# A decoder trunk on one core: a third pair of SwiGLU units by block products, and SiLU in one step

## The chip, the cores and the metric

One core of one Trainium2 chip runs the whole program in one launch. The metric is the device time of one execution in microseconds; smaller is better. Three runs of the kernel before were timed, and one more execution was profiled.

## What is computed

Four layers. Each is: half a SwiGLU, a token mixer (retention, sparse attention with an indexer, native sparse attention, retention) beside a four-head attention into 256 memory tokens, and half a SwiGLU again. There are 256 tokens of width 1024, all float32, and the hidden width of a SwiGLU is 2816. Only the SwiGLU is touched:

```python
def swiglu(x, wg, wu, wd):
    return (jax.nn.silu(x @ wg) * (x @ wu)) @ wd

h = rms_norm(x, ffn_norm[i, 0])
x = x + 0.5 * swiglu(h, ffn_w_gate[i, 0], ffn_w_up[i, 0], ffn_w_down[i, 0])
```

## The kernel before

**Tiles and precision.** The 256 tokens are two row tiles `t` of 128. Every matrix product is done three times in a reduced-precision float32 type (F32R): an operand is split into `hi`, a rounded copy made on ScalarE, and `lo`, the rest, a subtraction on VectorE. `mm3` (L307 to L311) multiplies hi by hi, hi by lo and lo by hi. Weights are split on the chip too: each raw block of 128 x 2048 becomes two halves of 128 x 1024 (`split`, L281 and L282).

**Units.** A SwiGLU's weights come in units, in the order of `FFN_ORDER` (L23): gate/up units `("g", u)`, each 1024 x 512 (256 gate columns and 256 up columns), and down units `("d", u)`, each 512 x 1024 (the last 256 x 1024). An ordinary unit has two raw blocks of 1 MB. Both row tiles use a unit one after the other: 48 matmuls of 512 columns.

**Pairs by block products.** For each `u` in `JOINT` (L26; 4 and 8), units `u` and `u + 1` are one "j" unit of four blocks b11, b21, b12, b22. The two row tiles, the two halves of the inner dimension and the two units form a 2 x 2 block product, which `joint` (L477) does in seven products in place of eight: 84 matmuls (lines L491 to L493) in place of 96, with sums of blocks before and sums of products after. The sums of the token side are made once per SwiGLU (`sums`, L431) and held as five `op` tiles until its last pair. `fetch_joint` (L211) builds t1 = b12 + b11: SP loads the two halves of b12 into `sum` tiles, and POOL's DMA adds b11 onto them as it lands (L229). Then b11, b22 and b21 are loaded plain. `split_joint` (L237) splits seven blocks into 14 halves, in the order b11, t1, t2, t3, b21, t4, b22, each by a copy on ScalarE (L253) and a subtraction on VectorE (L254). t2 = t1 + b22 and t4 = t2 + b21 are summed in place (L250). t3 = t2 - b11 is put into two `sum` tiles of its own (L247).

**Buffers.** There are three raw buffers (8 KB a partition), nine pairs of `hi`/`lo` halves (`HALVES`), nine 4 KB buffers with the tag a4, which `sum` and `op` tiles share, and two banks of PSUM each for `pg` and for `pj`/`pT`.

**What sets the order.** `load` (L182) chains all loads of weights on SP: each is issued after the one before it in the code, whichever buffer it waits for. Units are fetched and split in the order of the list; in each `tick` one or two halves are split. Within these bounds the program's order on each engine is fixed when it is built.

**After a gate/up unit** (`ffn`, L1244): with p holding gate and up columns, r the row's 1/rms and rh = r/2, r2 = r squared, ScalarE computes `th = tanh(rh * gate)` (L1265), VectorE `th = (th + 1) * gate` (L1266) and `h = th * r2 * up` (L1271). The factor of 2 that this leaves is taken back at the end of the SwiGLU, with 0.25 for 0.5 (L1298). Every two units, h is transposed and split into `hTh` and `hTl` (L1280, L1281), the operands of the down units. The order of a SwiGLU is then g0 to g3, d0, pair 4/5, d1, g6, g7, d2, pair 8/9, d3, g10, d5, d4.

Of the kernel before, what the change touches and what calls it, by code (L numbers as in the profile page):

```python
# [11 lines left out]
AF = mybir.ActivationFunctionType  # L12
OP = mybir.AluOpType
# [9 lines left out]
FFN_ORDER = [("g", 0), ("g", 1), ("g", 2), ("g", 3), ("d", 0), ("g", 4), ("g", 5), ("d", 1),  # L23
             ("g", 6), ("g", 7), ("d", 2), ("g", 8), ("g", 9), ("d", 3), ("g", 10), ("d", 5), ("d", 4)]

JOINT = (4, 8,)  # L26


C_CS, C_TRI, C_GI, C_DK, C_CM, C_ANY, C_CCS, C_BM = 0, 256, 384, 390, 396, 524, 525, 653
# [51 lines left out]
class Net:  # L81
# [48 lines left out]
    def plan(self):  # L130
        a = self.a

        def ffn(i, j):
            for kind, u in FFN_ORDER:
                if kind == "g" and u in JOINT:
                    self.units.append(("j", [a["gu"][i, j, u, 0], a["gu"][i, j, u, 1], a["gu"][i, j, u + 1, 0],
                                             a["gu"][i, j, u + 1, 1]], None))
                elif kind == "g" and u - 1 in JOINT:
                    continue
# [15 lines left out]
        for j, i in enumerate(self.layers):  # L155
            n = len(self.units)
            ffn(i, 0)
            for u in range(n, len(self.units)):
                both(u)
            if j == 0:  # L160
                memory(i)
            kind = i % 3
            names = {0: ["ret"] * 5, 1: ["dsa0", "dsa1", "dsa2", "dsa2"],
                     2: ["nsa0", "nsa0", "nsa0", "nsa1", "nsa2", "nsa3"]}[kind]
            seen = {}
            for n in names:
                u = seen[n] = seen.get(n, -1) + 1
                w = a[n]
                idx = (i // 3, u) if n == "ret" else (u,)
                self.units.append(("w", [w[idx + (0,)], w[idx + (1,)]], None))  # L170
                both(len(self.units) - 1)
            if j + 1 < len(self.layers):
                memory(self.layers[j + 1])
            for u in range(2):
                self.units.append(("w", [a["wout"][i, u, 0], a["wout"][i, u, 1]], None))
            n = len(self.units)
            self.seq += [(n - 2, 0), (n - 1, 0), (n - 2, 1), (n - 1, 1)]
            ffn(i, 1)
            for u in range(n, len(self.units)):
                both(u)  # L180
# [56 lines left out]
    def split_joint(self, u):  # L237
        nc = self.nc
        raw, parts = self.raw.pop(u), self.parts[u]
        parts.update({n: [] for n in ("b11", "t1", "t2", "t3", "b21", "t4", "b22")})  # L240
        half = lambda n, q: raw[n][:, 1024 * q:1024 * q + 1024] if n[0] == "b" else raw[n][q]

        def quarter(name, src, q, plus):
            x = half(src, q)
            if name == "t3":
                raw.setdefault("t3", []).append(self.t4([128, 1024], "sum"))
                nc.vector.tensor_sub(raw["t3"][q], x, half("b11", q))  # L247
                x = raw["t3"][q]
            elif plus:
                nc.vector.tensor_add(x, x, half(plus, q))  # L250
            hi = self.wp.tile([128, 1024], F32R, name="hi", tag="hi", bufs=HALVES)
            lo = self.wp.tile([128, 1024], F32R, name="lo", tag="lo", bufs=HALVES)
            nc.scalar.activation(hi, x, AF.Copy)  # L253
            nc.vector.tensor_sub(lo, x, hi.bitcast(F32))  # L254
            parts[name].append((hi, lo))

        for name, src, plus in (("b11", "b11", None), ("t1", "t1", None), ("t2", "t1", "b22"), ("t3", "t1", None),
                                ("b21", "b21", None), ("t4", "t1", "b21"), ("b22", "b22", None)):
            for q in range(2):
                self.splits.append((u, lambda name=name, src=src, q=q, plus=plus: quarter(name, src, q, plus)))  # L260
# [983 lines left out]
    def ffn(self, t, g, st):  # L1244

        nc = self.nc
        H, acc, nd = {}, None, 0
        X = self.X[t]
        for kind, ui in FFN_ORDER:
            u = yield  # L1250
            if not H:
                s, r, rh, r2 = st["n"]
            if kind == "g":
                r_, rh_, r2_ = r, rh, r2
                if u == 0:
                    p = self.first[t]
                elif isinstance(u, tuple):
                    p, (_, r_, rh_, r2_) = u
                else:
                    p = self.pB("pg")  # L1260
                    self.project(p, s, u)
                if t and ui == 0:
                    self.sums()
                th = self.t1([128, 256], "th")
                nc.scalar.activation(th, p[:, :256], AF.Tanh, scale=rh_)  # L1265
                nc.vector.scalar_tensor_tensor(th, th, 1.0, p[:, :256], op0=OP.add, op1=OP.mult)  # L1266

                if ui % 2 == 0:
                    h = self.t2([128, 512], "h")
                hs = h[:, ui % 2 * 256:ui % 2 * 256 + 256]  # L1270
                nc.vector.scalar_tensor_tensor(hs, th, r2_, p[:, 256:], op0=OP.mult, op1=OP.mult)  # L1271
                if ui % 2 or ui == 10:
                    n = 4 if ui % 2 else 2
                    hl = H[ui // 2] = [self.t2([128, 4, 128], f"hT{x}", F32R) for x in "hl"]

                    def turn(h=h, hl=hl, n=n):
                        c = self.pC("pT")
                        for k in range(n):
                            nc.tensor.transpose(c[:, k], h[:, k * 128:k * 128 + 128], self.ident)  # L1279
                        nc.scalar.activation(hl[0][:, :n], c[:, :n], AF.Copy)  # L1280
                        nc.vector.tensor_sub(hl[1][:, :n], c[:, :n], hl[0][:, :n].bitcast(F32))  # L1281

                    self.later(WAIT["h"], turn)
            else:
                pr = self.parts[u]
                if acc is None:
                    acc = self.pA("acc")
                nk = len(pr)
                for cb in range(2):
                    for k in range(nk):  # L1290
                        hl = H[ui]
                        wh, wl = pr[k]
                        o = cb * 512
                        self.mm3(acc[cb], hl[0][:, k], hl[1][:, k], wh[:, o:o + 512], wl[:, o:o + 512],
                                 nd == 0 and k == 0, nd == 5 and k == nk - 1)
                    if nd == 5:
                        xs = X[:, cb * 512:cb * 512 + 512]
                        nc.vector.scalar_tensor_tensor(xs, acc[cb], 0.25, xs, op0=OP.mult, op1=OP.add)  # L1298
                        if g is None:
                            nc.scalar.dma_start(self.a["out"][t * 128:(t + 1) * 128, cb * 512:cb * 512 + 512], xs)  # L1300
                        else:
                            (self.norm_half if g >= 8 else self.norm_kept)(t, g, cb, st)
                    if cb == 0:
                        self.tick()
                nd += 1
        if g is not None:
            self.norm_stats(t, st)
# [303 lines left out]
```

## Time and profile before

| what | value |
| --- | --- |
| median of 3 runs | 2041.11 us (2036.3 to 2041.76) |
| the profiled execution | 2034.82 us |
| its span, first to last instruction | 2033.0 us |
| TensorE, VectorE, ScalarE busy | 99%, 76%, 55% of the span |
| mean granted clock of TensorE | 0.998 of full speed |
| read from HBM | 365.84 MB |

The busy time of an engine is the union of its instructions' times. Matmuls are pipelined: a matmul of 512 columns shows as about 0.39 us, while the next one begins some 0.23 us after it, so paces are read from stretches and not from single matmuls. PEld is TensorE's weight load, which overlaps the matmuls. DVE, ACT, POOL and SP are VectorE, ScalarE, GpSimd and SyncE; SPq and POOLq mark DMAs that they issue. An arrow with a name, as in `<-ACT hi L253`, names what ended the idle time before an instruction.

### The profile page before, as it was taken

What the parts mean: (1) busy time and instruction counts of PE and PEld (TensorE: products, weight loads), DVE (VectorE), ACT (ScalarE), POOL (GpSimd) and SP (SyncE); (2) the same over time, 40 slices, a digit from 0 to 9 for tenths busy, and PEclk for the clock granted to TensorE, in tenths of its full rate; (3) what the DMA queues carried; (4) which work ended last, traced back from release to release, by engine and by line L of the source; (5) the groups of instructions that cost most, each with busy time, mean ns of one, the idle gap of its engine ahead of it and who ended that gap; (6) DMA issues with size and microseconds to landing.
All of it is one profiled execution on the core that took longest, in us unless ns stands there. A gap on an engine that the chain in (4) does not pass through costs nothing.

```text
span 2033.0 us, 25241 instructions
## 1 busy us (share of the span) xinstructions
PE 2004.1 (99%) x9486; PEld 1615.2 (79%) x9486; DVE 1554.8 (76%) x2241; ACT 1114.5 (55%) x1562; POOL 198.5 (10%) x317
## 2 busy tenths in 40 slices
PE   8999999999999999999999999999999999999999
PEld 6777777888888787888788788878888878778887
DVE  7877756888787787887788876668887878657875
ACT  5545555556555555655555554555555646545553
POOL 0000402000001022100000113220000000301000
PEclk9999999999999999999999999999999999999999
DMA  6656535565545533655556553135655566435553
GB/s 246 221 187 228 187 117 194 165 229 222 192 186 178 203 114 125 205 189 169 218 193 232 188 179 131 67 110 202 217 197 186 166 228 223 150 125 199 194 166 125
DMA packets 57770, 368.53 MB, mean 181 GB/s; under 512 B 6576, under 2 KB 6992, under 8 KB 18864
## 3 DMA queue, kind: packets, MB, share of 16 engines
q1 hardware_dynamic: 51696, 347.76, 46.3%
q0 software_dynamic: 4800, 17.19, 4.8%
q10 hardware_dynamic: 1152, 1.97, 0.3%
q8 instruction: 75, 1.23, 0.2%
q14 instruction: 47, 0.39, 0.1%
HBM read 365.84 MB, written 1.05 MB: 180 GB/s over the span
## 4 chain that ended last, share of the span: by engine, by line
PE 87%; DMA 5%; DVE 4%; ACT 1%; issue 1%; POOL 1%; SPq 0%; ACTq 0%; POOLq 0%; DVEq 0%
PE pg L309 8%; PE pg L311 8%; PE pg L310 8%; PE acc L310 8%; PE acc L311 8%; PE acc L309 8%; DMA sum<-gu 4%; PE pg L492 3%; PE pg L491 3%; PE pg L493 3%; PE p L309 3%; PE p L310 3%; PE p L311 3%; PE pT L1279 2%; PE pT L564 1%; PE po L309 1%
## 5 line engine op out<-in xcount | busy, mean ns | idle before, releaser
L282 DVE TENSOR_TENSOR lo<-raw,hi 128x1024 fp32r<-128x1024 f32 (+3 forms) x516 | 614.1, 1216 | 103.3 <-ACT hi L281 96.8
L281 ACT ACTIVATE hi<-raw 128x1024 fp32r<-128x1024 f32 (+3 forms) x516 | 527.3, 1046 | 187.0 <-PE pg L311 53.7
L309 PE MATMUL pg<-hi,sh 128*128 128x512 f32 x896 | 355.5, 397 | 4.5 <-ACT hi L1364 3.4
L310 PE MATMUL pg<-lo,sh 128*128 128x512 f32 x896 | 351.1, 392 | 0.7 <-DVE lo L1365 0.7
L311 PE MATMUL pg<-hi,sl 128*128 128x512 f32 x896 | 350.0, 391 | 0.0
L310 PE MATMUL acc<-lo,hTh 128*128 128x512 f32 x704 | 281.1, 403 | 0.5 <-DVE lo L282 0.3
L311 PE MATMUL acc<-hi,hTl 128*128 128x512 f32 x704 | 278.8, 400 | 0.0
L309 PE MATMUL acc<-hi,hTh 128*128 128x512 f32 x704 | 278.1, 399 | 0.0
L253 ACT ACTIVATE hi<-sum 128x1024 fp32r<-128x1024 f32 x128 | 132.3, 1058 | 166.8 <-PE acc L311 82.2
L309 PEld LDWEIGHTS pg<-hi,sh 128*128 128x128 f32 x896 | 168.5, 188 | 39.6 <-ACT hi L1364 4.8
L311 PEld LDWEIGHTS pg<-hi,sl 128*128 128x128 f32 x896 | 168.5, 188 | 35.5
L310 PEld LDWEIGHTS pg<-lo,sh 128*128 128x128 f32 x896 | 168.8, 188 | 35.1 <-DVE lo L1365 2.3
L254 DVE TENSOR_TENSOR lo<-sum,hi 128x1024 fp32r<-128x1024 f32 x128 | 154.4, 1227 | 42.0 <-ACT hi L253 39.9
L310 PEld LDWEIGHTS acc<-lo,hTh 128*128 128x128 f32 x704 | 132.7, 188 | 36.8 <-DVE lo L282 7.6
L1265 ACT ACTIVATE th<-pg,rh 128x256 f32<-128x256 f32 x128 | 60.3, 471 | 178.4 <-PE pg L311 173.0
L309 PEld LDWEIGHTS acc<-hi,hTh 128*128 128x128 f32 x704 | 132.9, 189 | 29.4 <-ACT hTh L1280 1.6
L311 PEld LDWEIGHTS acc<-hi,hTl 128*128 128x128 f32 x704 | 132.9, 189 | 26.1 <-DVE hTl L1281 0.2
L1266 DVE SCALAR_TENSOR_TENSOR th<-th,pg 128x256 f32<-128x256 f32 x128 | 53.5, 418 | 101.8 <-ACT th L1265 101.2
L254 DVE TENSOR_TENSOR lo<-raw,hi 128x1024 fp32r<-128x1024 f32 x96 | 114.6, 1223 | 16.5 <-ACT hi L253 16.3
L309 PE MATMUL p<-hi,sh 128*128 128x512 f32 (+4 forms) x320 | 125.2, 391 | 0.3 <-DVE dq_b L546 0.3
L311 PE MATMUL p<-hi,sl 128*128 128x512 f32 (+4 forms) x320 | 121.2, 379 | 0.0
L310 PE MATMUL p<-lo,sh 128*128 128x512 f32 (+4 forms) x320 | 120.9, 378 | 0.0
(345 smaller groups left out, 3180.1 us busy)
## 6 DMA issues: line engine op xcount, KB each, us to landing
raw<-gu SPq DMA_DIRECT2D x158, 1024.0 KB, 5.1
raw<-dn SPq DMA_DIRECT2D x88, 1024.0 KB, 4.8
raw<-ret SPq DMA_DIRECT2D x20, 1024.0 KB, 4.9
sum<-gu SPq DMA_DIRECT2D x32, 512.0 KB, 7.0
sum<-gu POOLq DMA_DIRECT2D x32, 512.0 KB, 9.5
raw<-wout SPq DMA_DIRECT2D x16, 1024.0 KB, 4.8
raw<-mkv SPq DMA_DIRECT2D x8, 1024.0 KB, 4.9
raw<-nsa SPq DMA_DIRECT2D x6, 1024.0 KB, 4.9
```

The costliest lines, as they stand in the source:

```text
L253: nc.scalar.activation(hi, x, AF.Copy)
L254: nc.vector.tensor_sub(lo, x, hi.bitcast(F32))
L281: nc.scalar.activation(hi, src, AF.Copy)
L282: nc.vector.tensor_sub(lo, src, hi.bitcast(F32))
L309: mm(out, ah, bh, start=start, stop=False)
L310: mm(out, ah, bl, start=False, stop=False)
L311: mm(out, al, bh, start=False, stop=stop)
L491: mm(bank, a[0][:, k], bh, start=first and k == 0, stop=False, skip_group_check=True)
L492: mm(bank, a[0][:, k], bl, start=False, stop=False, skip_group_check=True)
L493: mm(bank, a[1][:, k], bh, start=False, stop=k == 3, skip_group_check=True)
L1265: nc.scalar.activation(th, p[:, :256], AF.Tanh, scale=rh_)
L1266: nc.vector.scalar_tensor_tensor(th, th, 1.0, p[:, :256], op0=OP.add, op1=OP.mult)
```

## The change

A third pair, units 6 and 7, is done by block products: the order becomes g0 to g3, d0, pair 4/5, d1, pair 6/7, d2, pair 8/9, d3, g10, d5, d4. The third sum t3 overwrites b11's raw block and takes no `sum` tiles. ScalarE computes `silu(r * gate)` in one instruction, so VectorE's L1266 goes; the scale of h becomes r and the last factor 0.5.

```diff
-JOINT = (4, 8,)
+JOINT = (4, 6, 8,)
...
             if name == "t3":
-                raw.setdefault("t3", []).append(self.t4([128, 1024], "sum"))
-                nc.vector.tensor_sub(raw["t3"][q], x, half("b11", q))
-                x = raw["t3"][q]
+                nc.vector.tensor_sub(half("b11", q), x, half("b11", q))
+                x = half("b11", q)
...
                 th = self.t1([128, 256], "th")
-                nc.scalar.activation(th, p[:, :256], AF.Tanh, scale=rh_)
-                nc.vector.scalar_tensor_tensor(th, th, 1.0, p[:, :256], op0=OP.add, op1=OP.mult)
+                nc.scalar.activation(th, p[:, :256], AF.Silu, scale=r_)
...
-                nc.vector.scalar_tensor_tensor(hs, th, r2_, p[:, 256:], op0=OP.mult, op1=OP.mult)
+                nc.vector.scalar_tensor_tensor(hs, th, r_, p[:, 256:], op0=OP.mult, op1=OP.mult)
...
-                        nc.vector.scalar_tensor_tensor(xs, acc[cb], 0.25, xs, op0=OP.mult, op1=OP.add)
+                        nc.vector.scalar_tensor_tensor(xs, acc[cb], 0.5, xs, op0=OP.mult, op1=OP.add)
```

## Rows read from the trace of the kernel before

**Rows 1.** Head of the page, and its chain that ended last, by engine.

```profile
span 2033.0 us, 25241 instructions
...
PE 2004.1 (99%) x9486; PEld 1615.2 (79%) x9486; DVE 1554.8 (76%) x2241; ACT 1114.5 (55%) x1562; POOL 198.5 (10%) x317
...
PE 87%; DMA 5%; DVE 4%; ACT 1%; issue 1%; POOL 1%; SPq 0%; ACTq 0%; POOLq 0%; DVEq 0%
```

**Rows 2.** Busy time by stretch (start:end and length, us), mostly of the second SwiGLU.

```profile
core 0: us, PE busy (x) PEld busy (x) DVE busy (x) ACT busy (x) POOL busy (x), PEclk, DMA share, GB/s
...
337.60:522.30 184.70, 184.70 (x833) 149.18 (x832) 149.02 (x183) 101.88 (x127) 6.99 (x12) 1.00 0.57 200
...
395.30:409.00 13.70, 13.70 (x61) 11.26 (x60) 13.09 (x13) 10.85 (x13) 0.00 (x0) 1.00 0.32 105
...
412.75:418.30 5.55, 5.55 (x26) 4.55 (x25) 4.98 (x7) 3.87 (x5) 0.00 (x0) 1.00 0.92 304
...
395.30:426.90 31.60, 31.60 (x141) 25.32 (x140) 28.84 (x35) 20.80 (x26) 0.00 (x0) 1.00 0.57 207
...
426.90:449.20 22.30, 22.30 (x102) 18.41 (x101) 14.69 (x18) 10.57 (x14) 1.74 (x2) 1.00 0.89 282
...
461.00:492.50 31.50, 31.50 (x141) 25.26 (x140) 28.69 (x35) 20.87 (x26) 0.00 (x0) 1.00 0.55 210
...
383.70:395.30 11.60, 11.60 (x53) 9.39 (x53) 10.02 (x12) 3.96 (x5) 0.00 (x0) 1.00 0.21 72
...
62.00:79.40 17.40, 13.34 (x53) 10.44 (x52) 11.52 (x13) 6.92 (x11) 2.83 (x4) 0.90 0.58 220
```

**Rows 3.** Timeline of DVE around a pair's start at 395.3: start, length, us.

```profile
391.77 1.22 DVE L250 TENSOR_TENSOR sum<-sum,raw 128x1024 f32<-128x1024 f32 x1
...
394.57 3.50 DVE L254 TENSOR_TENSOR lo<-sum,hi 128x1024 fp32r<-128x1024 f32 x3 [1.58 <-ACT hi L253]
...
400.26 1.22 DVE L254 TENSOR_TENSOR lo<-sum,hi 128x1024 fp32r<-128x1024 f32 x1
...
401.39 1.22 DVE L250 TENSOR_TENSOR sum<-sum,raw 128x1024 f32<-128x1024 f32 x1
...
402.53 0.69 DVE L505 TENSOR_TENSOR s<-pg,s 128x512 f32<-128x512 f32 x1
...
407.23 4.63 DVE L282 TENSOR_TENSOR lo<-raw,hi 128x1024 fp32r<-128x1024 f32 x4
```

**Rows 4.** Groups by line, whole span: count, then busy us, mean ns, idle before.

```profile
L253 ACT ACTIVATE hi<-sum 128x1024 fp32r<-128x1024 f32 x128 | 132.3, 1058 | 166.8 <-PE acc L311 82.2 <-DVE sum L250 55.8 <-DMA sum<-gu 18.1
...
L1266 DVE SCALAR_TENSOR_TENSOR th<-th,pg 128x256 f32<-128x256 f32 x128 | 53.5, 418 | 101.8 <-ACT th L1265 101.2
...
L1266 DVE SCALAR_TENSOR_TENSOR th<-th,s 128x256 f32<-128x256 f32 x48 | 18.8, 419 | 0.0
...
L501 ACT ACTIVATE s<-pg 128x512 f32<-128x512 f32 x16 | 9.3, 578 | 0.0
```

**Rows 5.** Timeline of SP's and POOL's DMAs and of ACT, same SwiGLU.

```profile
391.92 11.08 SPq L184 DMA_DIRECT2D raw<-dn  x2
...
428.01 0.90 SPq L184 DMA_DIRECT2D sum<-gu  x2
...
434.83 0.87 POOL L229 DMA_DIRECT2D sum<-gu  x1 [66.46 <-DMA sum<-gu]
...
449.08 1.06 ACT L253 ACTIVATE hi<-sum 128x1024 fp32r<-128x1024 f32 x1 [1.36 <-DMA sum<-gu]
```

**Rows 6.** DMA issues, whole span: count, KB each, median us to landing.

```profile
raw<-dn SPq DMA_DIRECT2D x88, 1024.0 KB, 4.8
...
sum<-gu POOLq DMA_DIRECT2D x32, 512.0 KB, 9.5
```

**Rows 7.** Waits of SP's queue, 337 to 523 us: total us, times, longest.

```profile
SPq L184 <- DVE sum L250: 20.6, 2, 10.4
```

**Rows 8.** ACT's table load, from the groups by line: busy us, mean ns.

```profile
L1394 ACT ACT_TABLE_LOAD x1 | 1.3, 1283 | 5.6 <-DMA gains<-gains 5.6
```

## The prediction

> **What bounds the kernel now.** I read the head of the page first. TensorE is busy for 2004.1 of 2033.0 us, VectorE for 1554.8, ScalarE for 1114.5, and 87% of the chain that ended last lies on TensorE [rows 1]. So taking matmuls away pays, as long as their operands arrive in time. The second view is the busy time by stretch, in the FFN from 337.6 to 522.3. TensorE is busy there without a break for 184.70 us, VectorE for 149.02, 81% [rows 2]. But from 395.30 to 426.90, a pair by products (60 and 24 matmuls; a stretch's count includes a neighbour or two) and the down unit's 48, VectorE is busy for 28.84 of 31.60 us: 91%. Where a pair is multiplied, VectorE is nearly the second bound. The third view, the groups by line, says what its work is, and its timeline in what order and at what pace.
>
> **Matmuls taken away.** Units 6 and 7 now take 96 matmuls, 22.30 us. By products they take 84: a pair's 60 took 13.70 and its 24 took 5.55, together 19.25 us [rows 2]. That is 3.05 us per SwiGLU and 24.4 us for eight.
>
> **VectorE's work.** The third pair adds 6 `lo` subtractions (14 halves in place of 8), 6 sums of blocks and 5 sums of products per SwiGLU. In the timeline such operations of 1024 columns follow each other every 1.14 us (400.26 to 401.39 to 402.53), and a sum of products takes 0.69 [rows 3]. 12 x 1.14 + 5 x 0.69 = 17.1 us. SiLU in one step removes L1266, 53.5 + 18.8 us in all, 9.0 per SwiGLU [rows 4]. So 149.0 becomes about 157 of 181.6 us, 86%, which fits as a mean. ScalarE gains 6 copies near 1.06 us and one of 0.58 us [rows 4] in an FFN where it was busy for 101.88 of 184.70 us [rows 2]; I cost that at nothing. L1265 keeps its size and only changes function. The scale `r_` for `rh_`/`r2_` and 0.5 for 0.25 cost nothing.
>
> **In a row.** The third pair lies between the other two, so the slack that units 6 and 7 gave (VectorE 14.69 of 22.30 us [rows 2]) is gone. One period is now a pair and a down unit: 18 `lo` and 6 sums, 24 x 1.14 = 27.4; 5 sums of products, 3.4; two `hTl`, as wide as these, 1.4; four `h`, as wide as L1266 at 0.42, 1.7 (these last two estimated from such widths). That is 33.9 us of VectorE in 31.6 us of TensorE. It cannot work far ahead either: nine `hi`/`lo` buffers hold the down unit's four halves and five of the pair's 14.
>
> **The third sum over its raw block.** It costs no operation. It frees two `sum` buffers, so the next pair's b12 has room at once. But b11's buffer is now held until t3 is split, 398.0 in the example pair (end of the three `lo` at 394.57, 3.50 long [rows 3]), where the next down load went out at 391.92 [rows 5]. Such a load lands in 4.8 us [rows 6] and its first `lo` came at 407.23, so this delay hides behind the splits of b21 and b22. The last of VectorE's block sums, t4's second, ends at 401.39 + 1.22 = 402.6 as before.
>
> **The queue decides.** Loads go out on SP strictly in order. The queue's waits show it stuck behind VectorE's block sums, 10.4 us at most for L250 [rows 7]: the second down load needs b21's buffer, which t4's second sum gives back. Now the next pair's b12 stands right behind that load. Call its issue S. Before, S was 428.01 for a pair that began at 461.0 [rows 2]: POOL's accumulating DMA went out at 434.83 [rows 5] and lands in 9.5 us at the median [rows 6], so the first half of t1 was ready at S + 16.3; the second made ScalarE wait until 449.08, S + 21 [rows 5]. 33 us of lead hid this. The cover is gone for pairs 6 and 8. With the example pair (start 395.3) as the first of three:
> - Pair 6: S = 402.6, t1 ready at 418.9. From there to the end of the last split VectorE has 18 operations, 20.5 us, plus 1.1 for the first `hi` and about 2 for products' sums: 23.6, to 442.5. TensorE, starting the pair at 426.9, wants that half after six and a half products of 2.75 us, at 426.9 + 17.9 = 444.8. In time, 2.3 us to spare.
> - Pair 8: pair 6's second t4 sum is the 15th of those operations, so S = 418.9 + 1.1 + 17.1 + 1.4 = 438.5, t1 ready at 454.8, last split at 478.4. TensorE would want it at 458.5 + 17.9 = 476.4. Late by 2.0 us, even if VectorE never idles.
>
> VectorE does idle: 31.60 - 28.84 = 2.8 us in the example period [rows 2]. Over the two periods from 407 to 478 that is 5.6 us. The row doesn't tell idling for lack of a free buffer, which a late VectorE no longer meets, from idling between dependent steps; I take half. So 4.8 us lost per SwiGLU, at TensorE's wait for t2 and t4 of the third pair. Bounds: 0, if the order happens to bring t4's sum forward, and 2.0 + 5.6 = 7.6, where all of the idling stays. 8 x 4.8 = 38.4 us. POOL issues two more accumulating DMAs per SwiGLU, and only these chains wait for it. Another 1 MB is read per pair, which is small against what was moved.
>
> **Tables of ScalarE.** The trace has one table load, 1.283 us [rows 8], though Tanh and Exp both run. It cannot show whether Silu lives with Exp. Between nothing and a load at each of the eight changeovers (into and out of four mixers): 0 to 10.3 us if all lay open. Loads before an FFN lie beside ample ScalarE idle time; the four ahead of an attention's Exp may half show: 2.6 us, nearer to the lower end as TensorE is 99% busy. The Trainium skill (ScalarE: Activation LUTs, "Table sets: the hidden batching unit") speaks against the change: functions come in sets, its row for exp lists tanh and not Silu, and each switch is put at about 2.7 us. Eight switches by that price, all exposed, would be an estimate of 21 us where the row gives 10.3; the single load here agrees that tanh sits with exp.
>
> **Sum.** -24.4 + 38.4 + 2.6 = +16.6 us. The profiled execution took 2034.8 us (span 2033.0), so 2051.4; the median of the runs, 2041.1, stands 6.3 above it, and 2058 is the forecast for the median. About 0.3%, 6 us, is what a measurement of this kernel can tell from no change.
>
> **Rivals.**
> - *Matmuls pay.* The engines' orders are fixed when the program is built, and nothing forces t4's second sum behind b21 and t4's first split: it needs only t2's second split and t3's second sum. Put right behind t3, it brings S forward by three to four operations, 3.4 to 4.6 us for each pair in the row, and the lateness of pair 8 falls to nothing or little. It decides from S at 434 or earlier. For it: the first t4 sum did run early, at 391.77. Against: the second did not, at 401.39 [rows 3]. Time: 2041.1 - 24.4 + 0 to 1.5 x 8, 2017 to 2029.
> - *A draw.* VectorE idles hardly at all, 2 to 3 us lost per SwiGLU: 2041.1 - 24.4 + 16 to 24 + 2.6, 2035 to 2043.
> - *Both pairs late.* The second half of t1 lands at S + 21 each time, pair 6 loses its 2.3 us of room too, and waits slow the clock. One stretch shows such a price: the first down unit took 17.40 us at a granted clock of 0.90, with TensorE idle for 4.06, where 11.60 is usual [rows 2]: 5.8 us lost. Two of these in two of three SwiGLUs, 8 us on average: 2041 - 24 + 64 + 3 = 2084.
> - *Loads in the open.* If each of the eight table loads stops the chain for its 1.283 us, 7.7 more than I charged: 2066.
> - *It doesn't do what it says.* L1266 was nowhere on the chain's large entries, so removing it may give nothing; that is in the sum already, since it only makes room on VectorE.
>
> **Chances.** The forecast with its neighbours (slower by over 6 us) 0.40, both pairs late 0.06, loads in the open 0.04; the matmuls pay 0.35; a draw 0.15, of which 0.13 lies within 0.3% and 0.02 below. So faster 0.37, same 0.13, slower 0.50. The two signs hold nearly equal weight: the likeliest case's own range is 2040 (2.6 us lost each) to 2080 (7.6 lost); the stated one, 2022 to 2082, reaches into the first rival's.
>
> **What would show it.** Right: 84 matmuls a pair in three places per FFN; about 31.6 us between the starts of pairs 4 and 6, but 53 or more from the start of pair 6 to the end of pair 8 (50.9 without waits); in that last stretch VectorE over 95% busy and TensorE waiting for `lo` of L254 (t2, t4), and ScalarE's L253 for DMA `sum`; S of the third pair 20 us or less before its start. Nine table loads of 1.28 us. Wrong: TensorE without waits through all three pairs, or S of pair 8 more than 25 us ahead of it; VectorE idle in the row of pairs; or the loss at pair 6 or in the mixers instead.

## The result, and the profile after

The changed kernel takes 2187.24 us at the median of four runs (2181.41 to 2196.34), beside 2040.93 for the kernel before: a ratio of 1.0726, 95% interval 1.0683 to 1.0768. It is slower by 146 us, far beyond the 2082 that the forecast allowed. The profiled execution took 2196.34 us, the slowest of the four.

The head of the page after, with the chain by engine (answers to [rows 1]):

```profile
span 2194.6 us, 25064 instructions
...
PE 2040.4 (93%) x9390; PEld 1629.5 (74%) x9390; DVE 1622.0 (74%) x2201; ACT 1177.4 (54%) x1627; POOL 206.0 (9%) x333
...
PE 66%; DMA 14%; DVE 12%; ACT 4%; issue 3%; POOL 1%; SPq 0%; ACTq 0%; POOLq 0%; DVEq 0%
...
DMA sum<-gu 13%; DVE lo L253 6%; PE acc L310 6%; PE pg L310 6%; PE pg L309 6%; PE pg L308 6%; PE acc L309 6%; PE acc L308 5%; PE p L308 3%; PE p L310 3%; PE p L309 3%; PE pT L1277 2%; DVE lo L281 2%; ACT hi L252 2%; PE pg L490 2%
```

TensorE has 96 matmuls fewer and is idle for 154 us of the span, where it was idle for 29. The chain now runs for 13% of the time through POOL's accumulating DMA. (Lines of the changed kernel have numbers one or two lower than before: L252, L253 are the copy and subtraction of a pair, L246 and L249 its sums, L1264 SiLU, L1269 h. Each experiment shifts the numbers again; the names of the tiles tell the operations.)

The same SwiGLU by stretch (answers to [rows 2]): the whole, then each pair with the down unit behind it, then the end of the first down unit. The first number after the length is TensorE's busy time, then the weight loads', VectorE's, ScalarE's and GpSimd's, then the granted clock.

```profile
354.50:557.70 203.20, 187.23 (x822) 149.49 (x821) 157.61 (x178) 109.46 (x135) 8.69 (x14) 0.97 0.54 187
412.00:450.60 38.60, 33.10 (x141) 26.47 (x140) 29.67 (x33) 20.31 (x25) 1.73 (x2) 0.96 0.58 191
450.60:492.50 41.90, 34.52 (x142) 26.85 (x141) 32.05 (x34) 20.13 (x24) 1.74 (x2) 0.92 0.53 176
492.50:528.00 35.50, 32.41 (x141) 25.09 (x140) 32.98 (x36) 22.89 (x27) 0.00 (x0) 1.00 0.56 207
...
434.90:450.60 15.70, 10.20 (x42) 8.02 (x41) 9.16 (x12) 6.51 (x9) 0.00 (x0) 0.89 0.31 78
```

The SwiGLU takes 203.20 us where it took 184.70, and eight times 18.5 is 148, so nearly the whole loss lies here (the two profiled executions differ by 161.6 us of span). A pair with its down unit took 31.60 before. Now the three take 38.60, 41.90 and 35.50, 21.2 us too many. VectorE, by the forecast the tight engine, is busy for only 29.67 of 38.60 us in the first of these.

What stopped TensorE there, from the timelines of SP, POOL, ScalarE, VectorE and TensorE (start and length, us):

```profile
419.70 0.90 SPq L184 DMA_DIRECT2D sum<-gu  x2
...
426.76 0.86 POOL L229 DMA_DIRECT2D sum<-gu  x1 [41.58 <-DMA sum<-gu]
...
437.10 1.06 ACT L252 ACTIVATE hi<-sum 128x1024 fp32r<-128x1024 f32 x1 [5.01 <-DMA sum<-gu]
440.28 1.06 ACT L252 ACTIVATE hi<-sum 128x1024 fp32r<-128x1024 f32 x1 [2.13 <-DMA sum<-gu]
441.25 0.89 ACT L1264 ACTIVATE th<-s,rstd 128x256 f32<-128x256 f32 x2
...
438.19 1.22 DVE L253 TENSOR_TENSOR lo<-sum,hi 128x1024 fp32r<-128x1024 f32 x1 [4.03 <-ACT hi L252]
441.77 0.88 DVE L1269 SCALAR_TENSOR_TENSOR h<-th,rstd,s 128x256 f32<-128x256 f32 x2 [2.36 <-ACT th L1264]
...
442.40 1.09 PE L1277 MATMUL pT<-ident,h 128*128 128x128 f32 x4 [5.50 <-DVE h L1269]
443.14 0.78 PE L310 MATMUL acc<-hi,hTl 128*128 128x512 f32 x1
...
485.18 0.66 PE L1277 MATMUL pT<-ident,h 128*128 128x128 f32 x2 [5.45 <-DVE h L1269]
```

b12 of pair 6 goes out at 419.70, 7.7 us after pair 4 began (412.0). Its two halves of t1 reach ScalarE at 437.10 and 440.28, 17.4 and 20.6 us later. Both copies of t1 stand in ScalarE's queue ahead of the SiLU of pair 4's last results (441.25), and t1's subtraction stands in VectorE's queue ahead of their h (441.77). TensorE's order has the transposes of that h in the middle of down unit 1, so TensorE stops for 5.50 us, until 442.40, at a moment when its next operands for pair 6 are not even wanted. Then the matmul of 443.14 takes 0.78 us where 0.39 was usual: the granted clock of that stretch is 0.89. The same happens before pair 8 (5.45 us, until 485.18).

### The profile page after: what moved, and what is told of

Same layout as the page of the kernel before. It is cut to its first block, busy times and chain, and to the rows that moved or that the text cites. A ratio compares the mean times of both kernels' runs of the same rounds, so it can differ in the third digit from the quotient of the medians.

```text
span 2194.6 us, 25064 instructions
## 1 busy us (share of the span) xinstructions
PE 2040.4 (93%) x9390; PEld 1629.5 (74%) x9390; DVE 1622.0 (74%) x2201; ACT 1177.4 (54%) x1627; POOL 206.0 (9%) x333
## 3 DMA queue, kind: packets, MB, share of 16 engines
HBM read 374.23 MB, written 1.05 MB: 171 GB/s over the span
## 4 chain that ended last, share of the span: by engine, by line
PE 66%; DMA 14%; DVE 12%; ACT 4%; issue 3%; POOL 1%; SPq 0%; ACTq 0%; POOLq 0%; DVEq 0%
DMA sum<-gu 13%; DVE lo L253 6%; PE acc L310 6%; PE pg L310 6%; PE pg L309 6%; PE pg L308 6%; PE acc L309 6%; PE acc L308 5%; PE p L308 3%; PE p L310 3%; PE p L309 3%; PE pT L1277 2%; DVE lo L281 2%; ACT hi L252 2%; PE pg L490 2%
## 5 line engine op out<-in xcount | busy, mean ns | idle before, releaser
L281 DVE TENSOR_TENSOR lo<-raw,hi 128x1024 fp32r<-128x1024 f32 (+1 forms) x452 | 536.0, 1215 | 92.8 <-ACT hi L280 88.0
L280 ACT ACTIVATE hi<-raw 128x1024 fp32r<-128x1024 f32 (+1 forms) x452 | 459.2, 1043 | 147.4 <-PE pg L310 36.0
L252 ACT ACTIVATE hi<-sum 128x1024 fp32r<-128x1024 f32 x144 | 152.2, 1057 | 214.0 <-DMA sum<-gu 119.0
L308 PE MATMUL pg<-hi,sh 128*128 128x512 f32 x640 | 254.1, 397 | 4.6 <-ACT hi L1362 3.4
L253 DVE TENSOR_TENSOR lo<-raw,hi 128x1024 fp32r<-128x1024 f32 x192 | 227.3, 1218 | 32.5 <-ACT hi L252 32.5
L309 PE MATMUL pg<-lo,sh 128*128 128x512 f32 x640 | 250.6, 392 | 0.7 <-DVE lo L1363 0.7
L310 PE MATMUL pg<-hi,sl 128*128 128x512 f32 x640 | 250.9, 392 | 0.0
L253 DVE TENSOR_TENSOR lo<-sum,hi 128x1024 fp32r<-128x1024 f32 x144 | 175.0, 1220 | 92.1 <-ACT hi L252 91.2
L252 ACT ACTIVATE hi<-raw 128x1024 fp32r<-128x1024 f32 x192 | 193.2, 1050 | 87.5 <-DMA raw<-gu 61.3
L1277 PE MATMUL pT<-ident,h 128*128 128x128 f32 x352 | 74.2, 320 | 96.2 <-DVE h L1269 96.2
L1277 PEld LDWEIGHTS pT<-ident,h 128*128 128x128 f32 x352 | 50.9, 162 | 124.9 <-issue 106.9
L1264 ACT ACTIVATE th<-pg,rstd 128x256 f32<-128x256 f32 x104 | 49.1, 472 | 167.8 <-PE pg L310 109.7
L490 PE MATMUL pg<-hi,op 128*128 128x512 f32 x288 | 114.9, 399 | 15.5 <-DVE s L504 15.5
## 6 DMA issues: line engine op xcount, KB each, us to landing
sum<-gu POOLq DMA_DIRECT2D x48, 512.0 KB, 10.3
```

The costliest lines, as they stand in the source:

```text
L280: nc.scalar.activation(hi, src, AF.Copy)
L281: nc.vector.tensor_sub(lo, src, hi.bitcast(F32))
L308: mm(out, ah, bh, start=start, stop=False)
L309: mm(out, ah, bl, start=False, stop=False)
L310: mm(out, al, bh, start=False, stop=stop)
L490: mm(bank, a[0][:, k], bh, start=first and k == 0, stop=False, skip_group_check=True)
```

## The experiments

Theory A says that late block sums t1 of a pair that follows a pair cause the loss, with the previous pair's SiLU and h standing behind them. Theory B blames VectorE's work in the row; theory C the tables of Silu or b11's buffer. Ratios are against the kernel before, which ran beside each.

### The parts without the third pair

```diff
-JOINT = (4, 6, 8,)
+JOINT = (4, 8,)
```

> The changed kernel with two pairs (4 and 8), so SiLU in one step and t3 over b11 alone. Theory A (the late block sum t1 of a pair that follows another pair stops ScalarE and VectorE, whose queues hold the previous pair's SiLU and h behind it, and TensorE waits for the transposes of h): without a pair right behind a pair nothing is late, so 2041 us within 6, and the nine added table loads of 1.28 us hidden. Theory B (VectorE has too much work where three pairs stand in a row): the same, perhaps 0 to 8 less. Theory C (Silu's table loads, or b11's raw block held longer, cost the time): a good part of the 146 us stays, 2080 or more.

Measured: 2029.33 us, ratio 0.9957 (0.9944 to 0.997), below what A (2035) and B (2033) allowed. So neither SiLU nor t3 over its raw block costs anything with two pairs, and C is out as the cause. A later run had SiLU in one step alone, with t3 in `sum` tiles of its own (the scales that go with it, here and in the next experiment, are left out of the excerpts):

```diff
-                nc.scalar.activation(th, p[:, :256], AF.Tanh, scale=rh_)
-                nc.vector.scalar_tensor_tensor(th, th, 1.0, p[:, :256], op0=OP.add, op1=OP.mult)
+                nc.scalar.activation(th, p[:, :256], AF.Silu, scale=r_)
...
```

> The kernel before with SiLU in one step and nothing else. If the 0.43% that two pairs with SiLU and t3 over b11 gained is SiLU's (less VectorE work, a shorter chain from product to h): 2026 to 2034. If it comes from t3's buffers: 2036 to 2042. Nine more table loads than before in either case.

Measured: 2026.97 us, ratio 0.9947 (0.9932 to 0.9962). The gain of two pairs is SiLU's, and t3's place changes nothing that these intervals tell apart. The table loads are there, as groups by line of the two-pair run show (count, busy us, mean ns, idle before):

```profile
L1264 ACT ACT_TABLE_LOAD x5 | 6.4, 1283 | 7.2 <-PE pg L310 7.2
...
L600 ACT ACT_TABLE_LOAD x4 | 5.1, 1283 | 4.7 <-DVE nb L597 4.7
```

Nine more than before: five ahead of a first SiLU (one at the start), four ahead of a first Exp. So Silu and Exp need a switch here. The loads take 11.5 us of ScalarE's time, and the kernel is still 11 us faster.

### SiLU in two steps, with three pairs

```diff
-                nc.scalar.activation(th, p[:, :256], AF.Silu, scale=r_)
+                nc.scalar.activation(th, p[:, :256], AF.Tanh, scale=rh_)
+                nc.vector.scalar_tensor_tensor(th, th, 1.0, p[:, :256], op0=OP.add, op1=OP.mult)
...
```

> The changed kernel with SiLU in its old two steps (Tanh on ScalarE, then a VectorE operation), three pairs and t3 over b11 kept. Theory A: the waits for t1 stay, VectorE has about 9 us more per SwiGLU, part of it beside the waits: 2187 to 2230. Theory B: VectorE decides, so nearly all of 8 x 9 us shows: 2240 to 2260. Theory C (tables): 2160 or less, with one table load left.

Measured: 2237.78 us, ratio 1.0984 (1.0962 to 1.1005), just above A's range and below B's. The step is worth some 50 us here, four to five times what it is worth alone. That VectorE is on the path after every wait would explain it; no run tests that by itself.

### b12 loaded ahead of the down unit

```diff
+        if u and u + 1 < len(self.units) and self.units[u - 1][0] == self.units[u + 1][0] == "j":
+            self.start_joint(u + 1)
         self.raw[u] = []
...
+    def start_joint(self, u):
...
+        for q in range(2):
+            self.load(t1[q], half(b12, q))
+        for q in range(2):
+            self.nc.gpsimd.dma_start(t1[q], half(b11, q), accum_op=OP.add)
```

> The changed kernel, but the loads of b12 and the accumulating DMAs of a pair that follows another pair are put ahead of the down unit's loads between them on SP and POOL, so t1 is ready some 20 us sooner. Theory A: the two stalls of 7 to 8 us before pairs 6 and 8 vanish; what is left is VectorE's lag, at most 5 us per SwiGLU, against the 3.05 us gained: 2017 to 2060. Theory B: VectorE's work is unchanged, so most of the loss stays: 2130 or more. Theory C: no change, 2187.

Measured: 2046.92 us, ratio 1.0047 (1.0032 to 1.0062). One change of place, on SP's and POOL's queues, takes away some 140 of the 146 us. The head of its page, the three periods by stretch, and TensorE's longest waits in the whole span:

```profile
span 2043.3 us, 25104 instructions
...
PE 1992.6 (98%) x9390; PEld 1592.6 (78%) x9390; DVE 1618.3 (79%) x2201; ACT 1178.7 (58%) x1627; POOL 214.3 (10%) x333
```

```profile
391.60:423.20 31.60, 31.60 (x142) 25.29 (x141) 29.86 (x33) 20.37 (x25) 1.73 (x2) 1.00 0.70 229
423.20:456.60 33.40, 32.15 (x141) 25.19 (x140) 31.83 (x35) 21.16 (x25) 0.00 (x0) 1.00 0.46 161
456.60:491.40 34.80, 32.62 (x142) 25.16 (x141) 32.37 (x35) 21.95 (x27) 0.00 (x0) 1.00 0.57 212
```

```profile
PE acc L313 <- DVE lo L285: 11.6, 16, 1.4
PE pg L494 <- DVE s L508: 11.4, 16, 1.2
```

The first is back at 31.60. The others stay 1.8 and 3.2 us longer. There VectorE is busy for 31.83 of 33.40 and 32.37 of 34.80 us, and what TensorE waits for most are results of VectorE. That is the lag that the prediction had counted as 33.9 in 31.6, some 2 us smaller, now alone on the stage.

The two profiled executions also show the price of the slow clock. Their spans differ by 151.3 us at the same 9390 matmuls. TensorE is idle for 154.2 us in the changed kernel and for 50.7 here, which makes 103.5; the other 47.8 us are busy time, 2040.4 against 1992.6, at a mean granted clock of 0.969 against 0.999.

### t1 summed by VectorE

```diff
...
         start("t1")
-        add("t1", b11)
...
-        for name, src, plus in (("b11", "b11", None), ("t1", "t1", None), ("t2", "t1", "b22"), ("t3", "t1", None),
+        for name, src, plus in (("b11", "b11", None), ("t1", "t1", "b11"), ("t2", "t1", "b22"), ("t3", "t1", None),
```

> The changed kernel, but b11 is added to b12 by VectorE and not by POOL's accumulating DMA: t1 is ready about 10 to 11 us after b12's issue in place of 17 to 20, for two more VectorE operations of 1.14 us per pair (55 us in all). Theory A: the wait for t1 shrinks by 6 to 9 us at each of two places per SwiGLU, given back in part by VectorE: 2080 to 2150. Theory B: VectorE's added work makes it slower: 2210 to 2240.

Measured: 2081.32 us, ratio 1.0216 (1.0195 to 1.0236). With b12 as late as in the changed kernel, but without the accumulating DMA behind it, 106 us go, although VectorE has two more sums per pair. The first row is the period of pair 4, the second that of pair 6; below them b12's issue and the first copy of t1, with the SiLU behind it:

```profile
394.70:426.10 31.40, 31.40 (x141) 25.31 (x140) 30.10 (x33) 19.40 (x24) 0.00 (x0) 1.00 0.53 201
426.10:461.50 35.40, 32.62 (x142) 25.09 (x141) 34.05 (x37) 20.54 (x25) 0.00 (x0) 1.00 0.46 178
```

```profile
402.39 0.90 SPq L184 DMA_DIRECT2D sum<-gu  x2
...
415.06 1.06 ACT L247 ACTIVATE hi<-sum 128x1024 fp32r<-128x1024 f32 x1 [0.30 <-DVE lo L248]
416.03 0.89 ACT L1259 ACTIVATE th<-s,rstd 128x256 f32<-128x256 f32 x2
```

b12 goes out 7.7 us after the pair's start, as before, but t1's first copy comes 12.7 us after that in place of 17.4. A second way of making t1 sooner agrees with the first. It doesn't part lateness from standing in line, since only one of t1's copies still stands ahead of the SiLU in this run. The next one does.

### The order on two engines alone

The copies and subtractions of t1 are put behind the previous pair's last SiLU and h by an order edge; the DMAs keep their order.

```diff
...
             nc.scalar.activation(hi, x, AF.Copy)
+            if name == "t1" and self.last_th is not None:
+                self.behind(nc.cur_bb.bb.instructions[-1], self.last_th)
             nc.vector.tensor_sub(lo, x, hi.bitcast(F32))
+            if name == "t1" and self.last_th is not None:
+                self.behind(nc.cur_bb.bb.instructions[-1], self.last_h)
...
```

> The changed kernel, in which only the order on two engines is changed: the copies (ScalarE) and subtractions (VectorE) of t1 are put behind the previous pair's last SiLU and last h. The loads and t1's readiness stay as late as they are. Theory A1 (what costs most is the standing in line: SiLU, h and so the transposes wait behind an operation that waits for a DMA): TensorE no longer stops some 5.5 us before those transposes, and of 18.7 us lost per SwiGLU about half goes: 2080 to 2130. Theory A2 (the lateness of t1 by itself holds the pair up, whoever stands behind it): TensorE stops a little later instead, at the pair's t2: 2150 to 2190.

Measured: 2140.47 us, ratio 1.0504 (1.0483 to 1.0525): between the two ranges, 47 of 146 us back. The period of pair 4 and that of pair 6 by stretch, two stops of TensorE in the latter, and what it waited for in the whole span (us in total, times, longest):

```profile
406.00:437.50 31.50, 31.50 (x141) 25.36 (x140) 26.67 (x30) 18.23 (x23) 1.74 (x2) 1.00 0.71 234
437.50:479.00 41.50, 35.63 (x142) 27.14 (x141) 34.61 (x37) 21.79 (x26) 1.74 (x2) 0.92 0.53 177
```

```profile
449.58 0.50 PE L496 MATMUL pg<-lo,sh 128*128 128x512 f32 x1 [1.99 <-DVE lo L256]
...
454.43 1.20 PE L313 MATMUL acc<-hi,hTh 128*128 128x512 f32 x4 [2.05 <-ACT hi L285]
```

```profile
PE pg L496 <- DVE lo L256: 41.2, 24, 2.0
PE acc L313 <- ACT hi L285: 28.4, 16, 2.1
```

In the changed kernel the first wait on TensorE's list, and the largest one for a pair's own halves, were these:

```profile
PE pT L1277 <- DVE h L1269: 96.2, 18, 6.6
...
PE pg L491 <- DVE lo L253: 6.6, 8, 0.9
```

The standing in line is gone and the period of pair 4 is whole again. The period of pair 6 is as long as before, because its own halves now come too late: TensorE waits at the pair's products (pg, at 449.58 for b21's half) and then for the next down unit's halves (acc), whose copies stand behind the pair's on ScalarE. So both theories hold in part. The standing in line made the first stop of each SwiGLU, 47 us in all; the lateness as such keeps the second, and with it most of the loss. Loading b12 sooner removes both.

### What holds the row after that

Two tries at VectorE's remaining lag. First, t3's two sums on GpSimd, with b12 early:

```diff
-                nc.vector.tensor_sub(half("b11", q), x, half("b11", q))
+                nc.gpsimd.tensor_tensor(half("b11", q), x, half("b11", q), op=OP.subtract)
```

> The kernel with b12 loaded ahead of the down unit (2047 us), and the two sums of t3 per pair moved from VectorE to GpSimd, which is 9% busy: 2.3 us less of VectorE's 34 to 35 us per period. If VectorE's work is what holds the row of pairs, each of two periods per SwiGLU gets 2 to 3 us shorter: 2005 to 2025. If it is the chain from sum to copy to subtraction, or GpSimd slows VectorE, or its sums take longer than the chain has room for: 2040 to 2080.

Measured: 2073.78 us, ratio 1.0177 (1.0162 to 1.0192), slower than with VectorE. The group of these sums, and ScalarE's wait for the next sum in the same run; then one GpSimd sum and the VectorE sum beside it; then the group of VectorE's sums for t2 and t4 with b12 early, and in this run:

```profile
L250 POOL TENSOR_TENSOR raw<-sum,raw 128x1024 f32<-128x1024 f32 x48 | 120.2, 2507 | 258.4 <-DVE sum L253 227.4 <-ACT th L1268 18.9 <-DMA raw<-gu 12.1
...
ACT hi L256 <- DVE sum L253: 135.9, 62, 4.8
```

```profile
393.40 2.40 POOL L250 TENSOR_TENSOR raw<-sum,raw 128x1024 f32<-128x1024 f32 x1 [3.50 <-DVE sum L253]
...
393.78 3.11 DVE L253 TENSOR_TENSOR sum<-sum,raw 128x1024 f32<-128x1024 f32 x1
```

```profile
L253 DVE TENSOR_TENSOR sum<-sum,raw 128x1024 f32<-128x1024 f32 x96 | 116.7, 1215 | 0.0
...
L253 DVE TENSOR_TENSOR sum<-sum,raw 128x1024 f32<-128x1024 f32 x96 | 153.6, 1613 | 0.5 <-DMA raw<-gu 0.5
```

One takes 2.5 us, twice VectorE's 1.22, and it stands in the chain t2, t3, t4, which runs in turn: t3 reads the tile that t4 then overwrites. ScalarE's wait for those sums was 63.9 us with b12 early and t3 on VectorE. GpSimd also slows VectorE: the sum that begins at 393.78, beside one of GpSimd's, takes 3.11 us and ends 1.1 us after it. VectorE's busy time rises from 1618.3 to 1647.3 us, with 48 operations fewer. So VectorE did not become lighter at all, and this run can't tell whether less work there would help.

Second, more TensorE work between the pairs. Order g0 to g3, pair 4/5, d0, d1, pair 6/7, d2, d3, pair 8/9, g10, d5, d4:

```diff
-FFN_ORDER = [("g", 0), ("g", 1), ("g", 2), ("g", 3), ("d", 0), ("g", 4), ("g", 5), ("d", 1),
-             ("g", 6), ("g", 7), ("d", 2), ("g", 8), ("g", 9), ("d", 3), ("g", 10), ("d", 5), ("d", 4)]
+FFN_ORDER = [("g", 0), ("g", 1), ("g", 2), ("g", 3), ("g", 4), ("g", 5), ("d", 0), ("d", 1),
+             ("g", 6), ("g", 7), ("d", 2), ("d", 3), ("g", 8), ("g", 9), ("g", 10), ("d", 5), ("d", 4)]
```

> The kernel with b12 loaded early, in another order of units: g0 to g3, pair 4/5, d0, d1, pair 6/7, d2, d3, pair 8/9, g10, d5, d4, so that two down units (about 25 us of TensorE for 9 us of VectorE) stand behind each of the first two pairs. If VectorE's 34 us in 31.6 us is what is left of the loss, it vanishes (39 us in 44): 2005 to 2025. If it is the chain through t1's DMA or the raw buffers: 2035 or more.

Measured: 2049.54 us, ratio 1.0057 (1.004 to 1.0073), a miss. The stretches are those of pair 6 with two down units, and of pair 8 alone, up to the start of g10; below them TensorE's only large wait of that end:

```profile
429.60:472.20 42.60, 42.60 (x189) 34.35 (x188) 37.90 (x40) 25.06 (x30) 0.00 (x0) 1.00 0.47 173
472.20:496.70 24.50, 21.18 (x86) 16.90 (x85) 21.96 (x23) 16.10 (x19) 0.00 (x0) 0.93 0.64 235
```

```profile
PE pg L494 <- DVE s L513: 3.3, 1, 3.3
```

The middle pair runs without a wait, as hoped. The last pair stops at the product that must wait for VectorE's sum s3 to clear its bank. In the other orders a down unit, which has banks of its own, fills that gap; here only g10 follows, which needs a bank that the pair still holds.

So g10 was moved instead. Once with nothing else changed from the kernel with b12 early:

```diff
-             ("g", 6), ("g", 7), ("d", 2), ("g", 8), ("g", 9), ("d", 3), ("g", 10), ("d", 5), ("d", 4)]
+             ("g", 6), ("g", 7), ("d", 2), ("g", 10), ("g", 8), ("g", 9), ("d", 3), ("d", 5), ("d", 4)]
```

> The kernel with b12 loaded early (2047), with one change of order: g10 moved between d2 and pair 8/9, so that only the third pair gets a longer stretch before it and pair 6/7 still stands one down unit behind pair 4/5. If VectorE lags by 2 to 3 us in each of the periods in a row, the periods from pair 6/7 on get back what they lost, some 5 of the 5 to 6 us per SwiGLU, since pair 6/7 itself was on time: 2005 to 2025. If VectorE's lag is not what is left: 2040 or more.

Measured: 2022.9 us, ratio 0.9925 (0.9899 to 0.9951). And once with pair 4/5 also moved ahead of d0:

```diff
-FFN_ORDER = [("g", 0), ("g", 1), ("g", 2), ("g", 3), ("d", 0), ("g", 4), ("g", 5), ("d", 1),
-             ("g", 6), ("g", 7), ("d", 2), ("g", 8), ("g", 9), ("d", 3), ("g", 10), ("d", 5), ("d", 4)]
+FFN_ORDER = [("g", 0), ("g", 1), ("g", 2), ("g", 3), ("g", 4), ("g", 5), ("d", 0), ("d", 1),
+             ("g", 6), ("g", 7), ("d", 2), ("g", 10), ("g", 8), ("g", 9), ("d", 3), ("d", 5), ("d", 4)]
```

> Three pairs, b12 loaded early, SiLU in one step, and the order g0 to g3, pair 4/5, d0, d1, pair 6/7, d2, g10, pair 8/9, d3, d5, d4: two other units behind each of the first two pairs, and a down unit, which needs no bank of the pairs, behind the last. If VectorE's 34 us of work in a period of 31.6 us and the missing down unit behind the last pair are all that kept the third pair's 3.05 us per SwiGLU from showing: 24 us less than SiLU alone (2027), less one or two: 2000 to 2010. If the chain of sum, copy and subtraction inside a pair holds it up wherever it stands: 2025 or more.

Measured: 2007.32 us, ratio 0.9842 (0.9812 to 0.9873), the fastest of all, and faster than SiLU alone. Its head of page, and pair 6 with d2, then g10, then pair 8 with its down unit and the first matmuls of the next:

```profile
span 2005.8 us, 25107 instructions
...
PE 1978.1 (99%) x9390; PEld 1599.0 (80%) x9390; DVE 1615.7 (81%) x2201; ACT 1182.6 (59%) x1627; POOL 215.0 (11%) x333
```

```profile
423.50:455.10 31.60, 31.60 (x141) 25.29 (x140) 27.71 (x31) 21.16 (x26) 0.00 (x0) 1.00 0.64 233
455.10:466.30 11.20, 11.20 (x51) 9.19 (x51) 11.20 (x12) 6.15 (x8) 0.00 (x0) 1.00 0.00 1
466.30:500.00 33.70, 33.70 (x153) 27.53 (x152) 30.28 (x35) 23.13 (x28) 0.00 (x0) 1.00 0.62 222
```

TensorE has no idle time in any of the three, at the same number of matmuls and sums as the changed kernel: with b12 early the pairs are not too dear, only too close.

Three pairs with t3 in `sum` tiles of its own weren't tried: five `op` tiles, two of t3 and two for each of two pairs' t1 would be 11 of nine buffers. Spreading the pairs without loading b12 early wasn't tried either, so how much of the 2007 the order would give by itself stays open.

## Why the prediction was wrong

- **Matmuls taken away: right.** 3.05 us per SwiGLU, 24.4 in all. The spread order against SiLU alone, each by its ratio (0.9842 and 0.9947), is 1.05% of about 2037, 21 us, near enough for these intervals.
- **S and t1's readiness: right.** S was put 7.3 us after the first pair's start, t1's first half 16.3 and its second 21 after S. Measured: 7.7, and 17.4 and 20.6 for the copies. The ledger went on from the first half alone.
- **VectorE's work: nearly right in size.** 157 us in the SwiGLU were forecast, 157.61 came. A period's 33.9 was 2 us too high: with b12 early it is 31.83 and 32.37. SiLU's step makes room, as said.
- **The step that failed** is "Pair 6: ... In time, 2.3 us to spare". The ledger took t1's lateness to be harmless as long as the pair's last half was in time, and "only these chains wait for it" was all that it said of other users. It left out two things. First, what stands behind the instruction that waits: on ScalarE the SiLU of the pair before, on VectorE its h, and TensorE's fixed order needs the transposes of h in the down unit before pair 6. So TensorE stopped at 436.9, some 7 us before pair 6 was due (31.6 after 412.0). The order-only run puts 47 of the 146 us on this. Second, what TensorE wants besides the pair's last half: in that run this half was split 17.7 us after the pair's start, in time by the ledger's 17.9, but on the way TensorE stopped for b21's half and for the next down unit's. 4.8 us per SwiGLU was forecast to be lost and, with the 3.05 that the matmuls gave, 18.5 + 3.05 = 21.6 were. That the forecast said "slower" was luck in the main: the wait that it named, for t2 or t4 of the third pair, can be at most the 6.6 us that TensorE waited for all halves of pairs (L253), where 38.4 were charged.
- **Carried on from there.** In the ledger pair 8's t1 depends on pair 6's last block sum. So each delay of pair 6 moved S for pair 8, whose own stop followed (41.90 us for that period). The clock took its part too (0.96 and 0.92 in the two periods). The rival "both pairs late" had the shape, at 2084, but it priced a late pair at 5.8 us, where the first two periods lost 7.0 and 10.3, and spread that over two of three SwiGLUs.
- **Its signs of being wrong came.** S of the third pair was 462.25, 30 us ahead of its start at 492.5 and not 20 or less; VectorE was idle in the row; and the loss began at pair 6.
- **The tables: one load more than counted, and no cost that shows.** 2.6 us was set aside for eight more loads of 1.283 us; nine more came, and SiLU alone still is 11 us faster. So removing L1266, put at nothing by itself, is worth at least that. No run parts the two. The page of the Trainium skill that spoke against the change (ScalarE: Activation LUTs, "Table sets: the hidden batching unit") gives about 2.7 us for a load, which would have been an estimate of 24 for nine. The trace disagrees with that price, at 1.283 us for each load, and agrees that functions come in sets: one stands at each change between Silu and Exp. With SiLU alone one of them has no gap around it: the instruction before ends at 26.14, the one behind begins at 27.45.
- **t3 over its raw block: right**, no cost that can be measured with two pairs.
- **The rival "matmuls pay"** was thought to hang on the place of t4's sum in the order. It hangs on the place of b12 in SP's queue, and on the distance between pairs.

## What to carry to other kernels

When a transfer becomes late, list what stands behind the first instruction that waits for it, on every engine and in every queue; in kernels with a fixed order the cost can be set by the next unrelated result that another engine needs, and not by the slack of the late data's own last user. A load for a later stage that stands behind a load waiting for a buffer inherits that wait, so issue first what has a buffer free. And where one engine is short of time in a dense stretch, try moving stages apart before moving its work to a slower engine, which may also hold up the first.

## What the runs showed of the hardware

- A base load and an accumulating DMA onto it, 512 KB each, made a tile ready 17 to 21 us after the first issue. The accumulating part is 10.3 us at the median in the changed kernel and 6.8 with b12 early; why, no run shows.
- GpSimd's subtraction of 128 x 1024 float32 takes 2.5 us, VectorE's 1.22. A VectorE sum of the same size that began beside one took 3.11 us and ended 1.1 us after it.
- A switch between Silu and Exp costs ScalarE one table load of 1.283 us.
- After one stop of 5.5 us TensorE's next matmuls took 0.78 us in place of 0.39, the lower of its two clock levels (1.2 GHz), and the stretch's granted clock was 0.89. After the stop of 3.3 us at pair 8 in the run with two down units behind a pair, the stretch shows 0.93. With waits of at most 1.4 us, as in the run with b12 early, the granted clock stayed at 1.00 in the three periods. The run with the order alone shows 0.92 with stops of 1.99 and 2.05 us.
